# Attention value products issued for two key tiles at once, ahead of the sums of exp

## The chip, the cores and the metric

The kernel runs on one core of one Trainium2 chip. The metric is the device time of one execution in microseconds; smaller is better. Three executions before the change took 4082.6, 4084.34 and 4092.13 us; their median is 4084.34 us. A further execution was recorded by the hardware profiler; all rows of the profile come from it.

The engines are named as the profile names them: PE is TensorE (matmuls; PEld is its loading of weights), DVE is VectorE, ACT is ScalarE, POOL is GpSimd, SP is SyncE, which issues the DMAs.

## The reference

The program is a block of two layers over 1024 latent tokens and 256 context tokens, 1024 channels wide. Layer 0 mixes tokens with a bidirectional recurrence (RWKV-7), layer 1 with attention; each is followed by a squared-ReLU MLP. The change is in the attention of layer 1, which is cut here to what matters:

```python
sc = jnp.einsum('bqkgd,bskd->bkgqs', q, k_all) * scale   # 16 heads of 64, 4 key heads
p = jax.nn.softmax(sc, -1)                               # over 1024 + 256 keys
return jnp.einsum('bkgqs,bskd->bqkgd', p, v_all)
```

Only the 1024 latent tokens are queries; the keys are latent and context tokens, 1280 in all. So each head has 1024 queries, 10 key tiles of 128, and values 64 wide.

## The kernel before

All arithmetic is fp32. The dense layers split each operand into a high and a low part and make three matmuls of each product. Most of the time goes into these and into the recurrence; the attention of `phase_e` starts at about 2811 us of the span and ends at about 3253 us.

**Units and tiles.** `phase_e` (line 1319) goes over 16 units: 8 pairs of heads (`ct`) times 2 halves of 512 queries (line 1378). Within a unit it goes over the 10 key tiles (`kt`, line 1383). A key tile makes, in this order:

- scores: four matmuls, two for each head of the pair, into a PSUM tile of two banks (lines 1387 and 1388). The second of each pair has a 65th row that subtracts the row maximum, so exp needs no further operand;
- exp of the tile, on ScalarE, into an SBUF tile `p` (line 1391). `p` turns over five buffers (line 1389), so tile n+5 writes where tile n stood;
- the running sum of the `p` of a unit, `acc`, on GpSimd (lines 1396 and 1398; in the last pair of heads every third tile on VectorE);
- two "parts" (line 1402). In each part the generator `mx` is moved on by one (two while it catches up), and so is the generator `post`.

**Maxima.** `mx` is `maxima` (line 1200 on). It computes for later heads the row maxima that the scores subtract: one matmul pass into a PSUM bank (line 1224; two buffers) and one reduction on VectorE (lines 1226 and 1228). Once a unit it ends a head: a small reduction `mq` (line 1207), a transposing matmul `ps_mt` (line 1210), a ScalarE copy, and two DMAs. `MXLEAD = 6` and `MX0 = 4` set how far it runs ahead: in unit 0, from tile 2 on, it makes two steps in each part, later one, and in units 14 and 15 there are none left.

**Value products.** `values` (line 1341) makes the products of one key tile with the values: two calls, one for each head, whose outputs are 64 partitions each. They use half the columns of the array (`tile_position=(0, e * 64)`), and the profile shows four matmuls of the shape 128*64 for one key tile. They accumulate over the 10 key tiles in one PSUM bank, and ScalarE copies the result at the last one (line 1351). The tiles wait in the queue `late`; at line 1408 one is taken when more than `AVLAG = 2` stand there. So the products of tile n go out while tile n+2 is worked on.

**Sums and division.** `post` is `divided` (line 1353) for the unit before. It is started at tile `SUMAT = 3`. Its first step makes the matmul of `acc` with ones (line 1358), which also uses half the columns, and the first of eight reciprocals of 64 columns on VectorE (line 1361); each further part makes one more. Then come the product `ao * rec` (line 1363), a ScalarE copy (line 1366), and two parts later the low half `xl` (line 1369). The sum's PSUM buffer is one, shared with `ps_mt`.

**Order.** `line` (line 1335) chains what it is given: all matmuls of `phase_e` are one chain, and VectorE's reductions, reciprocals and products are another. Their order on the engine is therefore the order of the program's text. ScalarE and GpSimd follow their data. After the last unit, `late` is emptied and the last division is made (lines 1411 to 1413); then `phase_f` begins with the output projection.

Of the kernel before, what the change touches and what calls it, by code (L numbers as in the profile page):

```python
# [202 lines left out]
def drain(*gens):  # L203
    for g in gens:
        for _ in g:
            pass
# [980 lines left out]
def load_q(k, pools, ct):  # L1187

    nc, S, qs = k.nc, k.S, []
    for e in range(2):  # L1190
        o = slice(e * 64, e * 64 + 64)
        Q, Q2 = (pools[ct % len(pools)].tile([128, NL], F32R, name=f"{n}{e}", tag=f"{n}{e}") for n in ("Q", "M"))
        nc.sync.dma_start(out=Q[0:64].bitcast(F32), in_=S["qh"][ct][o])
        nc.sync.dma_start(out=Q[64:128].bitcast(F32), in_=S["ql"][ct][o])
        nc.sync.dma_start(out=Q2[0:64].bitcast(F32), in_=S["qh"][ct][o])
        qs.append((Q, Q2))
    return qs


def maxima(k, cts, qs, mp, pmx, psm, line):  # L1200


    nc, rows = k.nc, iter(())

    def row(ct, e, mc):
        m = mp.tile([128, 8], F32, name="mq", tag="mq")
        line(nc.vector.tensor_reduce(m, mc, AX.X, ALU.max), "v")
        yield
        ps = psm[0].tile([128, 512], F32, name="ps_mt", tag=psm[1])
        line(nc.tensor.matmul(ps[:8, :128], m, k.c["ident"], start=True, stop=True))  # L1210
        r = mp.tile([8, 128], F32R, name="mr", tag="mr")
        nc.scalar.activation(r, ps[:8, :128], AF.Copy, scale=-1.0)
        nc.sync.dma_start(out=k.S["mr"][ct][e].rearrange("(t q) -> t q", q=128), in_=r.bitcast(F32))
        nc.sync.dma_start(out=qs[ct][e][1][64:65].bitcast(F32), in_=k.S["mr"][ct][e:e + 1])

    for ct, e in itertools.product(cts, range(2)):
        Q, K_ = qs[ct][e][0], k.K1[ct // 2]
        mc = mp.tile([128, 8, 3], F32, name="mc", tag="mc")
        for t in range(0, 8, 2):
            for u, (t0, n) in [(u, b) for u in range(2) for b in TB[:2]] + [(None, TB[2])]:  # L1220
                ps = pmx[0].tile([128, 512], F32, name="ps_m", tag=pmx[1])
                for i in range(2) if u is None else (u,):
                    o = 256 * i if u is None else 0
                    line(nc.tensor.matmul(ps[:, o:o + n], Q[:, (t + i) * 128:(t + i) * 128 + 128], K_[:, t0:t0 + n], start=True, stop=True))  # L1224
                if u is None:
                    line(nc.vector.tensor_reduce(mc[:, t:t + 2, 2], ps.rearrange("p (a b) -> p a b", a=2), AX.X, ALU.max), "v")
                else:
                    line(nc.vector.tensor_reduce(mc[:, t + u, t0 // 512:t0 // 512 + 1], ps, AX.X, ALU.max), "v")  # L1228
                next(rows, None)
                yield  # L1230
        rows = row(ct, e, mc)
    drain(rows)
# [86 lines left out]
def phase_e(k, outs, qs, qp, mp):  # L1319

    tc, nc, S = k.tc, k.nc, k.S
    with ExitStack() as es:
        ep = es.enter_context(tc.tile_pool(name="ep", reuse_waits="tile", bufs=2))
        qp = (qp, *(es.enter_context(tc.tile_pool(name=f"qp{i}", reuse_waits="tile", bufs=1, side=side)) for i, side in ((1, "right"), (2, "left"))))
        pst = es.enter_context(tc.tile_pool(name="pst", reuse_waits="tile", bufs=2, space=PSUM))
        pmx = es.enter_context(tc.tile_pool(name="pmx", reuse_waits="tile", bufs=2, space=PSUM))
        psm = es.enter_context(tc.tile_pool(name="psm", reuse_waits="tile", bufs=1, space=PSUM))  # L1330
        pav = es.enter_context(tc.tile_pool(name="pav", reuse_waits="tile", bufs=1, space=PSUM))

        last = {}

        def line(i, e="pe"):

            if e in last:
                k.order(i, last[e])
            last[e] = i

        def values(u, p, kt, st):

            ct, half = u
            if kt == 0:
                st["av"] = pav.tile([128, 512], F32, name="ps_av", tag="av")
            for e in range(2):
                line(nc.tensor.matmul(st["av"][e * 64:e * 64 + 64], k.V[:, kt, ct // 2 * 64:ct // 2 * 64 + 64], p[:, e], start=(kt == 0), stop=(kt == 9),  # L1347
                                      tile_position=(0, e * 64)))
            if kt == 9:
                st["o"] = ep.tile([128, 512], F32, name="ao", tag="ao")  # L1350
                nc.scalar.copy(st["o"], st["av"])

        def divided(u, st):

            (ct, half), o = u, st["o"]
            ps = psm.tile([128, 512], F32, name="ps_su", tag="sm")
            for e in range(2):
                line(nc.tensor.matmul(ps[e * 64:e * 64 + 64], k.c["ones"][:, 0:64], st["acc"][:, e], start=True, stop=True, tile_position=(0, e * 64)))
            rec = ep.tile([128, 512], F32, name="rec", tag="rec", bufs=1)
            for j in range(0, 512, RW):  # L1360
                line(nc.vector.reciprocal(rec[:, j:j + RW], ps[:, j:j + RW]), "v")
                yield
            line(nc.vector.tensor_tensor(o, o, rec, ALU.mult), "v")
            sl = slice(half * 512, half * 512 + 512)
            hi, lo = outs[ct][0][:, sl], outs[ct][1][:, sl]
            nc.scalar.copy(hi, o)
            yield
            yield
            line(nc.vector.tensor_tensor(lo, o, hi.bitcast(F32), ALU.subtract), "v")
            if k.dbg and "ao" in k.O:  # L1370
                nc.sync.dma_start(out=k.O["ao"][ct][:, sl], in_=o)
            yield

        qs = {0: qs, **{ct: load_q(k, qp, ct) for ct in (1, 2)}}
        units = [(ct, half) for ct in range(KT) for half in range(2)]
        late, done, post, at, sent = collections.deque(), None, iter(()), 0, 0
        mx = maxima(k, range(1, KT), qs, mp, (pmx, "mx"), (psm, "sm"), line)
        for i, (ct, half) in enumerate(units):
            a, sl, st = ct // 2, slice(half * 512, half * 512 + 512), {}
            if half == 0:  # L1380
                if ct and ct + 2 < KT:
                    qs[ct + 2] = load_q(k, qp, ct + 2)
            for kt in range(10):
                ps = pst.tile([128, 2, 512], F32, name="ps_s", tag="s")
                kc = slice(kt * 128, kt * 128 + 128)
                for e, (Q, Q2) in enumerate(qs[ct]):
                    line(nc.tensor.matmul(ps[:, e], k.K1[a][:, kc], Q[:, sl], start=True, stop=False))  # L1387
                    line(nc.tensor.matmul(ps[:, e], k.K2[a][0:65, kc], Q2[0:65, sl], start=False, stop=True))  # L1388
                pool, tag = ((k.wp[1], "w_hi"), (k.wp[1], "w_lo"), (k.wp[0], "w_raw"))[(i * 10 + kt) % 5 % 3]
                p = pool.tile([128, 2, 512], F32, name="p", tag=tag)  # L1390
                nc.scalar.activation(p, ps, AF.Exp)  # L1391
                if kt == 0:
                    first = p
                elif kt == 1:
                    st["acc"] = ep.tile([128, 2, 512], F32, name="acc", tag="acc")
                    nc.gpsimd.tensor_tensor(st["acc"], first, p, ALU.add)
                else:
                    (nc.vector if ct == KT - 1 and kt % 3 == 2 else nc.gpsimd).tensor_tensor(st["acc"], st["acc"], p, ALU.add)  # L1398
                late.append(((ct, half), p, kt, st))
                if kt == SUMAT and i:  # L1400
                    post = divided(*done)
                for part in range(2):
                    at += 1
                    while sent < min(at + MXLEAD, 2 * (at - MX0)):
                        next(mx, None)
                        sent += 1
                    next(post, None)
                    if part == 0 and len(late) > AVLAG:
                        values(*late.popleft())
            done = (ct, half), st  # L1410
        while late:
            values(*late.popleft())
        drain(divided(*done))
# [3 lines left out]
AVLAG = 2  # L1417
# [63 lines left out]
```

## Time and profile before

| | us |
|---|---|
| median of three executions | 4084.34 |
| the profiled execution | 4093.04 |
| its span, first to last instruction | 4091.3 |
| PE busy in the span | 3611.4 (88%) |
| DVE busy | 2195.9 (54%) |
| ACT busy | 1512.4 (37%) |
| POOL busy | 1480.2 (36%) |
| value products, line 1347, 540 matmuls between 2811 and 3200 us | 145.8 busy |
| running sums, line 1398 on POOL, 109 adds there | 264.5 busy |

A row of the timeline gives the start, the duration, the engine, the line, the operation, output and inputs by the program's names, shapes, and how many were merged; in brackets the idle time of the engine before it and what ended it. Matmuls are pipelined, so the durations of neighbouring ones overlap: what one of them costs is read from start to start. A row of the windows gives a stretch, its length, the busy time and number of instructions of PE, PEld, DVE, ACT and POOL, the granted clock of TensorE as a share of full speed, the busy share of the DMA engines and GB/s.

### The profile page before, as it was taken

How to read it: one execution, taken by the hardware profiler on the slowest of the kernel's cores; microseconds unless marked ns; L12 is line 12 of the kernel's file. 1: busy time of each engine (PE TensorE's matmuls, PEld its weight loads, DVE VectorE, ACT ScalarE, POOL GpSimd, SP SyncE). 2: the span in 40 equal slices, each digit the busy share in tenths (PEclk: the TensorE clock that was granted, in tenths of full speed). 3: DMA queues.
4: the chain of work that ended last, by engine and by line, in shares of the span. 5: the costliest groups of instructions: out<-in, count | busy, mean ns of one | idle time of the engine just before them, and what ended most of it. 6: DMA issues, size and time to landing. Idle time of an engine off the chain costs nothing.

```text
span 4091.3 us, 70381 instructions
## 1 busy us (share of the span) xinstructions
PE 3611.4 (88%) x28100; PEld 2802.6 (69%) x28100; DVE 2195.9 (54%) x3707; ACT 1512.4 (37%) x3223; POOL 1480.2 (36%) x1387
## 2 busy tenths in 40 slices
PE   5999766883666779999999999889999999999998
PEld 3667654663566558788888888675444477888886
DVE  6337789998544665533333334657666453333334
ACT  5765555453444443411111112433444422221122
POOL 3114775765332423211111111124787612222221
PEclk7999866885878789999999999999999999999999
DMA  7456777777666553311111111432110111111112
GB/s 280 145 195 165 167 175 172 164 169 198 164 171 184 155 146 85 126 42 39 37 42 37 37 37 60 150 89 88 32 32 16 57 42 47 47 44 49 52 52 67
DMA packets 380279, 414.73 MB, mean 101 GB/s; under 512 B 150944, under 2 KB 280224, under 8 KB 374704
## 3 DMA queue, kind: packets, MB, share of 16 engines
q1 hardware_dynamic: 378992, 408.93, 36.4%
q8 instruction: 221, 3.62, 0.4%
q0 software_dynamic: 960, 1.31, 0.2%
q14 instruction: 106, 0.87, 0.1%
HBM read 294.99 MB, written 117.11 MB: 101 GB/s over the span
## 4 chain that ended last, share of the span: by engine, by line
PE 64%; DVE 11%; issue 4%; DMA 4%; ACT 1%; POOL 1%; SPq 1%; DVEq 0%; POOLq 0%; ACTq 0%
PE ps_pj L271 44%; PE ps_av L1347 4%; PE ps_s L868 3%; PE ps_m L1224 2%; PE ps_s L1387 2%; PE ps_pj L290 2%; PE ps_s L1388 2%; PE ps_y L877 1%; DVE To L712 1%; DVE Tn L713 1%; PE ps_x L848 1%; PE ps_x L854 1%; DMA wmod<-in_wmod 1%; DVE sgw L630 1%; DVE KT L653 0%
## 5 line engine op out<-in xcount | busy, mean ns | idle before, releaser
L255 POOL TENSOR_TENSOR w_lo<-w_raw,w_hi 128x512 fp32r<-128x512 f32 (+1 forms) x292 | 478.9, 1641 | 1677.7 <-ACT w_hi L253 1657.6
L271 PE MATMUL ps_pj<-xh,w_hi 128*128 128x512 f32 (+1 forms) x1712 | 626.3, 367 | 5.2 <-ACT w_hi L253 4.9
L271 PE MATMUL ps_pj<-xh,w_lo 128*128 128x512 f32 (+1 forms) x1712 | 618.3, 365 | 7.1 <-POOL w_lo L255 7.0
L271 PE MATMUL ps_pj<-xl,w_hi 128*128 128x512 f32 (+1 forms) x1712 | 622.6, 364 | 0.0
L1105 DVE SCALAR_TENSOR_TENSOR xr<-ps_pj,c_mod,xr 128x512 f32<-128x512 f32 (+1 forms) x368 | 251.8, 686 | 567.0 <-PE ps_pj L271 566.2
L253 ACT CAST w_hi<-w_raw 128x512 fp32r<-128x512 f32 (+1 forms) x292 | 216.6, 742 | 826.0 <-PE ps_pj L271 618.5
L271 PE MATMUL ps_pj<-hid_l,w_hi 128*128 128x512 f32 (+1 forms) x1280 | 474.4, 371 | 0.0
L271 PE MATMUL ps_pj<-hid_h,w_hi 128*128 128x512 f32 (+1 forms) x1280 | 473.1, 371 | 0.0
L271 PE MATMUL ps_pj<-hid_h,w_lo 128*128 128x512 f32 (+1 forms) x1280 | 469.8, 370 | 0.0
L1129 DVE TENSOR_TENSOR m_q<-m_r 128x512 f32<-128x512 f32 x160 | 183.6, 1149 | 415.5 <-ACT m_r L1127 415.2
L271 PEld LDWEIGHTS ps_pj<-xh,w_hi 128*128 128x128 f32 x1712 | 324.7, 190 | 59.9 <-ACT w_hi L253 6.6
L271 PEld LDWEIGHTS ps_pj<-xh,w_lo 128*128 128x128 f32 x1712 | 322.8, 190 | 61.0 <-POOL w_lo L255 9.9
L271 PEld LDWEIGHTS ps_pj<-xl,w_hi 128*128 128x128 f32 x1712 | 324.4, 190 | 51.5 <-issue 1.4
L1398 POOL TENSOR_TENSOR acc<-acc,p 128x1024 f32<-128x1024 f32 x122 | 295.5, 2423 | 58.6 <-ACT p L1391 54.2
L271 PEld LDWEIGHTS ps_pj<-hid_h,w_hi 128*128 128x128 f32 x1280 | 241.4, 189 | 44.3
L271 PEld LDWEIGHTS ps_pj<-hid_h,w_lo 128*128 128x128 f32 x1280 | 241.1, 188 | 43.8
L271 PEld LDWEIGHTS ps_pj<-hid_l,w_hi 128*128 128x128 f32 x1280 | 241.4, 189 | 43.2
L1391 ACT ACTIVATE p<-ps_s 128x1024 f32<-128x1024 f32 x160 | 163.8, 1024 | 231.1 <-PE ps_s L1388 229.2
L271 PE MATMUL ps_pj<-xhi,w_hi 128*128 128x512 f32 (+1 forms) x576 | 228.6, 405 | 15.2 <-ACT xhi L479 9.6
L271 PE MATMUL ps_pj<-xlo,w_hi 128*128 128x512 f32 (+1 forms) x576 | 227.2, 395 | 8.3 <-DVE xlo L480 8.1
L1228 DVE TENSOR_REDUCE mc<-ps_m 128x1 f32<-128x512 f32 x256 | 174.7, 690 | 100.8 <-PE ps_m L1224 97.0
L271 PE MATMUL ps_pj<-xhi,w_lo 128*128 128x512 f32 (+1 forms) x576 | 222.4, 388 | 3.7 <-POOL w_lo L255 3.7
(236 smaller groups left out, 6813.9 us busy)
## 6 DMA issues: line engine op xcount, KB each, us to landing
ST<-d_ST SPq DMA_DIRECT2D x40, 1152.0 KB
wmod<-in_wmod SPq DMA_DIRECT2D x32, 1024.0 KB
w_raw<-in_m SPq DMA_DIRECT2D x64, 512.0 KB
w_raw<-in_m SPq DMA_DIRECT2D x128, 256.0 KB
d_ST<-AR SPq DMA_DIRECT2D x160, 128.0 KB
d_LS<-KT SPq DMA_DIRECT2D x320, 64.0 KB
d_ST<-G SPq DMA_DIRECT2D x160, 128.0 KB
LS<-d_LS SPq DMA_DIRECT2D x80, 256.0 KB
```

Source lines behind the costliest of these rows:

```text
L253: nc.scalar.copy(hi, raw)
L255: getattr(nc, eng).tensor_tensor(lo, raw, hi.bitcast(F32), ALU.subtract)
L271: i = nc.tensor.matmul(ps[:, :n], w[:, sl], x[:, t0:t0 + n], start=a, stop=z)
L290: nc.tensor.matmul(ps[:, :n], w[:, sl], x[:, t0:t0 + n], start=a, stop=z)
L868: nc.tensor.matmul(pst[h * 64:h * 64 + 64, ct2, d, :], ls[:, h, ln, d, ct2, :, c], sv(h, ct2, d), start=True, stop=True, tile_position=(0, ...
L1105: k.nc.vector.scalar_tensor_tensor(x[:, t0:t0 + n], ps[:, :n], g, x[:, t0:t0 + n], ALU.mult, ALU.add)
L1129: nc.vector.tensor_tensor(q[:, :n], r[:, :n], r[:, :n], ALU.mult)
L1224: line(nc.tensor.matmul(ps[:, o:o + n], Q[:, (t + i) * 128:(t + i) * 128 + 128], K_[:, t0:t0 + n], start=True, stop=True))
L1228: line(nc.vector.tensor_reduce(mc[:, t + u, t0 // 512:t0 // 512 + 1], ps, AX.X, ALU.max), "v")
L1347: line(nc.tensor.matmul(st["av"][e * 64:e * 64 + 64], k.V[:, kt, ct // 2 * 64:ct // 2 * 64 + 64], p[:, e], start=(kt == 0), stop=(kt == 9) ...
L1391: nc.scalar.activation(p, ps, AF.Exp)
L1398: (nc.vector if ct == KT - 1 and kt % 3 == 2 else nc.gpsimd).tensor_tensor(st["acc"], st["acc"], p, ALU.add)
```

## The change

The call of `values` moves ahead of the step of `post`, and it is made at odd key tiles only, where it takes tiles from `late` until two are left. The matmuls, their number and their operands stay as they are.

```diff
                     while sent < min(at + MXLEAD, 2 * (at - MX0)):
                         next(mx, None)
                         sent += 1
+                    if part == 0 and kt % 2:
+                        while len(late) > AVLAG:
+                            values(*late.popleft())
                     next(post, None)
-                    if part == 0 and len(late) > AVLAG:
-                        values(*late.popleft())
```

On TensorE an even tile is then scores, maximum, maximum, and an odd tile is scores, maximum, value products of the two tiles two and three back, at tile 3 the sum of exp of the unit before, maximum. The last two tiles of a unit go out at tile 1 of the next, as they did at tiles 0 and 1; at the end the same two are left over.

## The prediction

> **What bounds the kernel now.** I read the page's span and chain first, then the busy time over the twelve middle units of the attention (the windows view), then TensorE's timeline there.
>
> ```profile
> span 4091.3 us, 70381 instructions
> ...
> 2858.84:3188.76 329.92, 329.92 (x1321) 160.72 (x1320) 226.93 (x372) 139.14 (x157) 261.84 (x109) 1.00 0.11 25
> ```
>
> The columns of the second row are the stretch, its length, busy time of PE, PEld, DVE, ACT and POOL, the granted clock, DMA. From the sum of exp of unit 1 to that of unit 13 TensorE is never idle (329.92 of 329.92 us, clock 1.00); VectorE has 227 and GpSimd 262 us of work. 12 units make one unit 27.49 us, a key tile 2.75. Everything outside the attention is untouched, so the whole question is what these 16 units become.
>
> Now one key tile on TensorE (start, duration, engine, line, what):
>
> ```profile
> 2958.04 0.40 PE L1224 MATMUL ps_m<-K,Q 128*128 128x256 f32 x2
> 2958.36 1.08 PE L1347 MATMUL ps_av<-p,Vat 128*64 128x512 f32 x4
> 2959.37 0.50 PE L1224 MATMUL ps_m<-K,Q 128*128 128x512 f32 x1
> 2959.71 0.39 PE L1387 MATMUL ps_s<-Q,K 128*128 128x512 f32 x1
> 2959.94 0.40 PE L1388 MATMUL ps_s<-M,K 65*128 65x512 f32 x1
> 2960.18 0.40 PE L1387 MATMUL ps_s<-Q,K 128*128 128x512 f32 x1
> 2960.42 0.40 PE L1388 MATMUL ps_s<-M,K 65*128 65x512 f32 x1
> 2960.66 0.40 PE L1224 MATMUL ps_m<-K,Q 128*128 128x512 f32 x1
> 2960.98 1.08 PE L1347 MATMUL ps_av<-p,Vat 128*64 128x512 f32 x4
> ```
>
> Durations overlap (the pipeline), so I count starts. Matmuls on the whole array (128*128) follow each other every 0.24 us (2959.71 to 2960.66 is four of them). The one ahead of the value products takes 0.32, the four value products on half the columns (128*64) 1.01, the maximum behind them 0.34. A block of value products that has another such block beside it is cheaper; the end of the attention and the step with the sum of exp show it:
>
> ```profile
> 3249.47 2.79 PE L1347 MATMUL ps_av<-p,Vat 128*64 128x512 f32 x12
> ```
>
> ```profile
> 2968.49 0.40 PE L1224 MATMUL ps_m<-K,Q 128*128 128x512 f32 x1
> 2968.82 1.08 PE L1358 MATMUL ps_su<-acc,c_ones 128*64 128x512 f32 x4
> 2969.73 1.03 PE L1347 MATMUL ps_av<-p,Vat 128*64 128x512 f32 x4
> 2970.68 0.50 PE L1224 MATMUL ps_m<-K,Q 128*128 128x512 f32 x1
> ```
>
> Three blocks in a row last 2.79, one lasts 1.08: each further block costs (2.79 - 1.08) / 2 = 0.855. The sum and its neighbour take 1.86 from start to the next maximum where two lone blocks take 2.02. So part of a lone block's price is the passage from the one shape to the other and back.
>
> **The change part by part.** *Fewer passages.* Maximum, lone block, maximum take 2958.04 to 2959.71 = 1.67; without passages they would take 2 x 0.24 + 0.855 = 1.33. One passage there and back costs 0.34. Before, a unit has 10 runs of half-column blocks (one for each key tile; the sum shares one with a value block). After, value products go out at odd tiles only, two tiles at once, and the sum at tile 3 stands behind them: 5 runs. That saves 5 x 0.34 = 1.70 a unit. Units 1 to 14: 14 x 1.70 = 23.8 us. No instruction is added or removed; no DMA moves.
>
> *Unit 0* loses. There the maxima catch up (four in a tile), and TensorE waits for VectorE:
>
> ```profile
> 2816.12 1.08 PE L1347 MATMUL ps_av<-p,Vat 128*64 128x512 f32 x4
> 2825.14 1.39 PE L1224 MATMUL ps_m<-K,Q 128*128 128x512 f32 x2 [7.94 <-DVE mc L1228]
> ```
>
> ```profile
> 2829.02 1.92 PE L1347 MATMUL ps_av<-p,Vat 128*64 128x512 f32 x4
> 2830.87 0.73 PE L1224 MATMUL ps_m<-K,Q 128*128 128x512 f32 x2
> ```
>
> ```profile
> 2825.00:2828.00 3.00, 2.86 (x6) 2.11 (x7) 1.97 (x4) 0.00 (x0) 1.70 (x1) 0.50 0.89 247
> ```
>
> The block of tile 0 stands ahead of that 7.94 us wait, for nothing. It moves behind it, where the clock is granted at half (0.50) and a block takes 2830.87 - 2829.02 = 1.85. Then tiles 4 and 6 have four maxima in a row with two PSUM buffers and no value products between them: the third waits for the first's reduction. By the durations below it comes 0.44 + 0.69 + 0.04 = 1.17 after the first and the fourth some 0.6 later, where 0.48 and 0.72 would do: about 1.1 of stall each. Against it stand 4 x 0.34 = 1.36 for its own four merged pairs and the short stalls that the catching-up has today. I take a loss of 2.0; the ends are a loss of 1.85 + 2.2 = 4 and a gain of 1.4.
>
> *VectorE.* Two tiles take 2 x 2.62 = 5.24 now and 4.90 then. VectorE's order stays (reduction, reciprocal, reduction, ...), but what it waits for moves.
>
> ```profile
> 2968.93 0.69 DVE L1228 TENSOR_REDUCE mc<-ps_m 128x1 f32<-128x512 f32 x1 [0.49 <-PE ps_m L1224]
> 2969.95 0.56 DVE L1361 RECIPROCAL rec<-ps_su 128x64 f32<-128x64 f32 x1 [0.33 <-PE ps_su L1358]
> 2971.23 0.69 DVE L1228 TENSOR_REDUCE mc<-ps_m 128x1 f32<-128x512 f32 x1 [0.72 <-PE ps_m L1224]
> 2971.84 0.55 DVE L1361 RECIPROCAL rec<-ps_su 128x64 f32<-128x64 f32 x1
> 2972.40 0.69 DVE L1226 TENSOR_REDUCE mc<-ps_m 128x2 f32<-128x512 f32 x1
> ```
>
> A reduction starts 0.44 after its maximum (2968.49 to 2968.93), 0.55 behind a run (2970.68 to 2971.23). Reduction to reciprocal is 0.61, reciprocal to reduction 0.56: in the tiles with reciprocals (3 to 6) VectorE needs 4 x 1.17 = 4.68 for two tiles. It fits 4.90 with 0.2 to spare, before 0.56. Where it is tight: at even tiles two maxima stand together. The second needs the buffer of the maximum behind the run, which started 0.34 + 0.95 + 0.24 = 1.53 earlier and is reduced 0.55 + 0.69 after its start, released 0.04 later (rows below: 2824.41 + 0.69 to 2825.14), 1.28 in all: spare 0.25. At tile 3 the first reciprocal comes 1.13 after the sum starts (2968.82 to 2969.95), the maximum 0.95 after it, and its reduction 1.13 + 0.56 - 0.95 = 0.74 behind the maximum: spare 0.06. So no stall, barely. What queues behind a late reduction is the maximum, and behind that, in TensorE's order, everything.
>
> *The lock between VectorE and GpSimd* is what can make VectorE late. A VectorE operation on two SBUF tiles waits for a running GpSimd add:
>
> ```profile
> 2821.59 2.34 POOL L1396 TENSOR_TENSOR acc<-p 128x1024 f32<-128x1024 f32 x1 [2.86 <-ACT p L1391]
> 2822.00 2.48 DVE L1308 TENSOR_TENSOR q_l<-q_n,q_h 128x512 fp32r<-128x512 f32 x1 [0.74 <-ACT q_h L1307]
> 2824.01 2.68 POOL L1398 TENSOR_TENSOR acc<-acc,p 128x1024 f32<-128x1024 f32 x1
> 2824.41 1.27 DVE L1228 TENSOR_REDUCE mc<-ps_m 128x1 f32<-128x512 f32 x2
> ```
>
> ```profile
> L1363 DVE TENSOR_TENSOR ao<-ao,rec x16: 679/681/2649, 2871.0 to 3258.0; 128x512 f32<-128x512 f32 x16
> L1369 DVE TENSOR_TENSOR xl<-ao,xh x16: 677/681/2097, 2874.0 to 3259.4; 128x512 fp32r<-128x512 f32 x16
> ```
>
> The q_l that is otherwise 0.69 took 2.48 and ended after the add; the queued add then waited (2.68 in place of 2.38). The two such operations of each unit, L1363 and L1369 at tiles 7 and 8, have a median of 0.681: today they fall into GpSimd's pauses. After, exp comes in pairs, the pauses move.
>
> ```profile
> 2960.91 1.02 ACT L1391 ACTIVATE p<-ps_s 128x1024 f32<-128x1024 f32 x1 [1.59 <-PE ps_s L1388]
> ```
>
> ```profile
> 2980.85 0.17 DVE L1207 TENSOR_REDUCE mq<-mc 128x8 f32<-128x24 f32 x1
> 2980.94 0.68 DVE L1363 TENSOR_TENSOR ao<-ao,rec 128x512 f32<-128x512 f32 x1
> ```
>
> By the count above L1363 falls due 10.6 after the sum starts (1.13 + 0.56 + 7 x 1.17 + 0.61, and 0.09 for the small L1207), that is 4.4 after the scores of tile 6 start (0.95 + 0.34 + 4.90 = 6.19 after the sum). The add of tile 6 begins about 2.4 after those scores (exp starts 1.20 after their first matmul, 2959.71 to 2960.91, and lasts 1.02) and ends at 4.8: a wait of 0.4, within the spare there. I take 0.1 a unit for it and the tight place together, 1.3 for units 1 to 13. The ends: 0, and a random phase. GpSimd will be busy 261.84 / 12 = 21.8 of 25.8 us, 85%; of a wait spread evenly over 0 to 2.4 the part beyond the spare of 0.25 is 2.15 x 2.15 / (2 x 2.4) = 0.96 on average, times 0.85 is 0.82, two of them 1.64 a unit, 21 us in all.
>
> The Trainium skill (SBUF — State Buffer, Who interferes with whom) says that a VectorE instruction with two SBUF inputs contends with a GpSimd instruction that reads SBUF, and that whoever issues first holds the port for its whole instruction. By that rule, the rows above agree (2.48 for 0.69); it is the rule that speaks against moving exp into pairs.
>
> *GpSimd and exp.* Two adds take 2 x 2.40 (261.84 / 109) = 4.80 of 4.90, nine of ten tiles have one: 21.8 of 25.8 a unit. It keeps up. The exp of tile n+5 reuses the p of tile n; an even tile's value products now run at n+3, still two tiles ahead. The copy of the accumulator gets a tile more. These cost nothing while that cover holds; without it a late p stops scores, and at most the 1.70 are gone.
>
> *Unit 15* and the end. The sum now starts 2 x 0.855 = 1.71 later in its step, and the reciprocals, L1363 and VectorE's add of tile 5 behind it:
>
> ```profile
> 3240.41 2.65 DVE L1363 TENSOR_TENSOR ao<-ao,rec 128x512 f32<-128x512 f32 x1
> 3242.98 1.21 DVE L1398 TENSOR_TENSOR acc<-acc,p 128x1024 f32<-128x1024 f32 x1
> ...
> 3244.71 2.37 POOL L1398 TENSOR_TENSOR acc<-acc,p 128x1024 f32<-128x1024 f32 x1 [2.21 <-ACT p L1391]
> ```
>
> GpSimd's add has 0.52 to spare after VectorE's (3244.19 to 3244.71). The scores of tile 3 come 0.34 + 0.855 = 1.2 earlier, the add 1.71 - 0.52 = 1.2 later against them, and the last sum and the next stage hang on it: 0, between a loss of 2.4 (one more add to wait for) and a gain of 1.7.
>
> **The sum.** 23.8 - 2.0 - 1.3 + 0 = 20.5 us. The profiled execution took 4093.04 (span 4091.3 and 1.74 around it): 4072.5. It lies 8.7 above the median of the runs, 4084.34: for the median 4084.34 - 20.5 = **4064**.
>
> **The rivals.** (a) *VectorE eats it.* The spare of 0.06 to 0.25 is missed and the lock comes at a random phase: 23.8 - 2 - 21 = 1 us of gain, 4084. For it: 85% of GpSimd's time; against it: the count that puts L1363 at the end of an add. (b) *Slower: both lock waits whole.* If L1363 and L1369 each start just behind a GpSimd add, in every unit, each waits 2.4, of which 2.15 reaches TensorE through the next maximum: 4.3 a unit against 1.70 saved, 13 x 2.6 = 34 lost, 2 more in unit 0 and 1.70 won in unit 14: 4084 + 34 = 4118. It decides once the two waits together pass 2.2 a unit. For it: 2649 and 2097 ns in the rows; against it: units repeat with one phase and the phase I find is another. (c) *It does not do what it says*: the passage is paid for each accumulation group rather than each change of shape, or GpSimd's pace sets the unit. Then nothing is saved, and unit 0 loses 2.0 + 1.36 = 3.4: 4088. Against it: the run of 12 and the sum beside a value block. (d) *Everything fits*: 23.8 + 1.4 + 1.7 = 27 us, 4057. (e) A run of half-column blocks might overlap its two column halves, so that each further block cost 0.43: 79 runs x 0.43 more, 34 us, 4030. Against it: 0.855 in the run of 12, whose blocks alternate the halves already.
>
> The Trainium skill (TensorEngine Tiling (Array Packing), Key Properties) says that different tiles can run matmuls in parallel; by that rule (e) would come. The trace disagrees, 0.855 for four matmuls.
>
> **How the numbers follow.** Forecast (gains of 13 to 24) 0.72, (d) 0.08, (a) 0.11, (b) 0.04, (c) 0.04, (e) 0.01. Runs of before lie between 4082.6 and 4092.13, and about 0.3% (12 us) is what a measurement tells from no change. Faster: 0.72 + 0.08 + 0.01 = 0.81. Same: (a) and (c), 0.15. Slower: 0.04. The range goes from (d) less 4 of scatter, 4053, to a gain of 6, 4078.
>
> **What would show it.** Right: pairs of value products as x8 of some 1.94, a unit of 25.8 between sums, the maxima behind one another 0.24 apart, L1363 still near 0.68 to 1.1. Wrong: TensorE idle before maxima on the release of a reduction in units 1 to 13, L1363 or L1369 with medians above 2, a marginal block above 1.0, a first unit longer by over 4.

## The result, and the profile after

The changed kernel takes 4055.01 us (median of four executions, 4051.38 to 4062.47), the kernel before 4086.53 beside it (4082.6 to 4092.13). The ratio of runs taken beside each other, which is not the quotient of the two medians, is 0.9934, with a 95% interval of 0.9917 to 0.9951: a gain of 20 to 34 us. A second timing, of both kernels unchanged, gave 4066.66 (five executions) against 4088.72 (fifteen): 0.9939, interval 0.9925 to 0.9952. The forecast was 4064, a gain of 20.5.

First the span and the windows view of the changed kernel from the sum of exp of unit 1 to that of unit 13, columns as before the change (stretch, length, busy time and instructions of PE, PEld, DVE, ACT, POOL, then granted clock, DMA share, GB/s).

```profile
span 4056.6 us, 70381 instructions
...
2850.12:3159.24 309.12, 309.12 (x1323) 168.92 (x1321) 219.81 (x372) 139.55 (x156) 262.98 (x109) 1.00 0.11 27
```

TensorE is still never idle in these twelve units and the clock is still 1.00, but they take 309.12 us in place of 329.92: 25.76 a unit in place of 27.49, 1.73 less. The instructions are the same. Now two key tiles and the step with the sum, in TensorE's timeline of the changed kernel (start, duration, engine, line, what).

```profile
2941.63 1.94 PE L1347 MATMUL ps_av<-p,Vat 128*64 128x512 f32 x8
...
2944.78 0.63 PE L1224 MATMUL ps_m<-K,Q 128*128 128x512 f32 x2
2945.24 0.39 PE L1387 MATMUL ps_s<-Q,K 128*128 128x512 f32 x1
...
2946.51 1.94 PE L1347 MATMUL ps_av<-p,Vat 128*64 128x512 f32 x8
...
2951.37 1.94 PE L1347 MATMUL ps_av<-p,Vat 128*64 128x512 f32 x8
2953.14 1.03 PE L1358 MATMUL ps_su<-acc,c_ones 128*64 128x512 f32 x4
```

The eight value matmuls stand as one run of 1.94 us, and from run to run are 2946.51 - 2941.63 = 4.88 us, where two tiles took 2 x 2.62 = 5.24 before. The maxima of an even tile stand together: two of them take 2945.24 - 2944.78 = 0.46, at the pace of 0.24 each that any full-array matmul has.

Where the whole gain lies is read from three places: the end of TensorE's long wait in unit 0, the first scores of unit 1, and the last sum of exp. For the changed kernel:

```profile
2815.11 1.39 PE L1224 MATMUL ps_m<-K,Q 128*128 128x512 f32 x2 [8.93 <-DVE mc L1228]
...
2840.82 0.40 PE L1387 MATMUL ps_s<-Q,K 128*128 128x512 f32 x1
...
3214.41 3.65 PE L1347 MATMUL ps_av<-p,Vat 128*64 128x512 f32 x16
3220.08 1.08 PE L1358 MATMUL ps_su<-acc,c_ones 128*64 128x512 f32 x4 [2.02 <-POOL acc L1398]
```

For the kernel before, whose wait ended at 2825.14:

```profile
2849.74 0.39 PE L1387 MATMUL ps_s<-Q,K 128*128 128x512 f32 x1
...
3253.33 1.08 PE L1358 MATMUL ps_su<-acc,c_ones 128*64 128x512 f32 x4 [1.06 <-POOL acc L1398]
```

From the wait to the last sum are 404.97 us in place of 428.19: the attention gains 23.2. From the last sum to the end of the span 836.52 in place of 837.97, 1.5 more. The change is therefore worth 24.7 us in these profiles. The spans differ by 34.7, and the other 10.0 lie ahead of the attention, where not a single instruction differs; the first experiment is about them.

| part | before | after | gain |
|---|---|---|---|
| end of the wait to first scores of unit 1 | 24.60 | 25.71 | -1.1 |
| first scores to sum of exp, unit 1 | 9.10 | 9.30 | -0.2 |
| sum of unit 1 to sum of unit 13 | 329.92 | 309.12 | 20.8 |
| sum of unit 13 to the last sum | 64.57 | 60.84 | 3.7 |
| last sum to the end of the span | 837.97 | 836.52 | 1.5 |

The second and the fourth row belong together: the sum of exp now stands behind one value block more (0.855) than before, which lengthens the way to the sum of unit 1 and shortens the way from that of unit 13.

### The profile page after: what moved, and what is told of

Read it like the earlier page. It is cut to its first block, busy times and chain, and to the rows that moved or that the text cites. A ratio compares the mean times of both kernels' runs of the same rounds, so it can differ in the third digit from the quotient of the medians.

```text
span 4056.6 us, 70381 instructions
## 1 busy us (share of the span) xinstructions
PE 3579.7 (88%) x28100; PEld 2807.2 (69%) x28100; DVE 2189.7 (54%) x3707; ACT 1510.9 (37%) x3223; POOL 1486.1 (37%) x1387
## 4 chain that ended last, share of the span: by engine, by line
PE 64%; DVE 11%; issue 4%; DMA 4%; ACT 1%; POOL 1%; SPq 0%; DVEq 0%; POOLq 0%; ACTq 0%
PE ps_pj L271 44%; PE ps_av L1347 4%; PE ps_s L868 3%; PE ps_m L1224 2%; PE ps_s L1387 2%; PE ps_pj L290 2%; PE ps_s L1388 2%; PE ps_y L877 1%; DVE To L712 1%; DVE Tn L713 1%; PE ps_x L854 1%; PE ps_x L848 1%; DVE sgw L630 1%; DVE KT L653 0%; DMA wmod<-in_wmod 0%
## 5 line engine op out<-in xcount | busy, mean ns | idle before, releaser
L830 POOL TENSOR_TENSOR T<-ST,c_qmask 128x256 f32<-128x256 f32 x160 | 118.2, 740 | 269.5 <-PE ps_x L854 187.0
```

Source lines behind the costliest of these rows:

```text
L830: k.nc.gpsimd.tensor_tensor(self.T, t.to_broadcast([128, 2, 4, 32]), k.c["qmask"].unsqueeze(1).to_broadcast([128, 2, 4, 32]), ALU.mult)
```

## The experiments

The theory, A: a unit is short by the passages between matmuls on half the columns and matmuls on the whole array, 0.34 us for each run of half-column blocks that is saved, and VectorE, GpSimd and the lock between them cost nothing as long as VectorE has its work done in 4.9 us for two tiles. The rivals: the order of the sums is what helps; the buffers of exp decide; VectorE is at its limit already.

**Both kernels again, unchanged: how much of the difference is the change?**

> The kernel before, unchanged, profiled a second time. The profiled execution of the changed kernel reached its attention 10 us earlier than that of the kernel before, though the change is behind that point. Theory A (scatter between executions): the second profile of the kernel before reaches its first scores anywhere within some 10 us of 2811, also near 2801, and its time lies anywhere between 4080 and 4095. Theory B (a property of the changed program): it reaches them again near 2811, within 2 us. Unit of the attention 27.49 us under both.

> The changed kernel, unchanged, timed in more rounds and profiled a second time. Theory A (scatter): its attention begins within some 10 us of 2801, and the difference to the kernel before comes nearer to the 23 us that the attention itself has gained in the first two profiles: ratio about 0.9943. Theory B (property of the program): attention begins again at 2801 within 2 us and the ratio stays at 0.992. Unit 25.76 us under both.

The kernel before came to 4086.74 against itself at 4088.72, ratio 0.9994 (0.9985 to 1.0004). The end of the long wait in unit 0 in the second profile of the kernel before, and in the second of the changed one:

```profile
2814.61 1.39 PE L1224 MATMUL ps_m<-K,Q 128*128 128x512 f32 x2 [7.60 <-DVE mc L1228]
```

```profile
2819.32 1.39 PE L1224 MATMUL ps_m<-K,Q 128*128 128x512 f32 x2 [8.81 <-DVE mc L1228]
```

The unchanged kernel now reaches the attention at 2814.61 where it took 2825.14 the first time, and the changed one at 2819.32 where it took 2815.11. So the 10.0 us are scatter of identical code, and in the second pair they have the other sign: spans 4080.9 and 4060.6 differ by 20.3, which is 25.0 less 4.7. Most of it arises in the recurrence: the 2560 matmuls of line 848 start between 1027.5 and 1479.0 us in the first profile of the kernel before and between 1027.3 and 1470.5 in its second, 451.5 against 443.2 us for the same instructions. From the wait to the last sum, on the other hand, the second profiles give 428.25 and 404.79, within 0.2 of the first. Below, a kernel is therefore judged by its unit (from sum to sum over twelve units), which repeats to 0.02 us: 27.493 and 27.493 before, 25.760 and 25.742 after. Several of the kernels below ran only once, under the profiler; their total time says little, their unit does.

**Value products on the whole array, in both orders: is it the change of shape?** If the gain is passages between shapes, it must vanish when the value products have the shape of everything else.

```diff
-                line(nc.tensor.matmul(st["av"][e * 64:e * 64 + 64], k.V[:, kt, ct // 2 * 64:ct // 2 * 64 + 64], p[:, e], start=(kt == 0), stop=(kt == 9),
-                                      tile_position=(0, e * 64)))
+                line(nc.tensor.matmul(st["av"], k.V[:, kt, ct // 4 * 128:ct // 4 * 128 + 128], p[:, e], start=(kt == 0 and e == 0), stop=(kt == 9 and e == 1)))
```

> The kernel before with value products on all 128 columns of the array (the values of two key heads side by side, both query heads into one PSUM bank, so the attention's result is another one). The sum of exp keeps its half columns. Theory (the price is the change of shape): of 10 runs of half-column blocks a unit 1 is left, 9 x 0.34 = 3.1 us less; the four matmuls of a tile follow each other at 0.235 in place of 0.214, 10 x 0.085 = 0.85 more: unit 27.49 - 3.1 + 0.85 = 25.3. Rival (the price is that of a block of value products that begins, whatever its shape): unit 27.5 to 28.3.

> The changed kernel with the same value products on all 128 columns (another result, as there). Theory (the price is the change of shape): of 5 runs 1 is left, 4 x 0.34 = 1.4 less, 0.85 more: unit 25.76 - 1.4 + 0.85 = 25.25, the same as in the other order of the products, so that the pairs bring nothing. Rival (a block that begins): 25.8 to 26.6, and the difference of 1.7 to the other order stays.

Both kernels leave out the separation of the two heads and so compute another attention; they serve for the time alone. They have one line less, so the scores stand in line 1386 and the sum in 1357. The windows of twelve units, with the order of before and with that of the change:

```profile
2866.53:3262.05 395.52, 395.52 (x1321) 231.53 (x1321) 227.09 (x372) 140.58 (x157) 261.06 (x109) 1.00 0.09 21
```

```profile
2864.79:3259.75 394.96, 394.96 (x1321) 231.26 (x1321) 219.80 (x372) 140.71 (x156) 260.07 (x109) 1.00 0.09 21
```

32.96 and 32.91 us a unit: the two orders differ by 0.05 where they differed by 1.73. Timed, they are level too (ratios to the kernel before 1.0201 and 1.0215, intervals 1.0184 to 1.0219 and 1.0201 to 1.0229). So the gain hangs on the change of shape. The size was missed: 25.3 was expected and 33 came. TensorE's timeline of the first of the two says why.

```profile
2952.59 0.40 PE L1224 MATMUL ps_m<-K,Q 128*128 128x256 f32 x2
2952.83 1.88 PE L1347 MATMUL ps_av<-p,Vat 128*128 128x512 f32 x4
2954.14 0.79 PE L1224 MATMUL ps_m<-K,Q 128*128 128x512 f32 x1
2954.77 0.40 PE L1386 MATMUL ps_s<-Q,K 128*128 128x512 f32 x1
```

From the maximum to the scores are 2.18 us, and less the two maxima of 0.24 the block costs 1.70, about twice the 0.855 of a block on half columns. The passage is gone: a maximum ahead of it takes 0.24, not 0.32. The four matmuls of a half-column block, then, run two at a time, one on each half of the columns, and in the whole-array form one after the other. The timeline merges neighbouring records; taken singly, over the first 0.4 us of a block (2958.40 to 2958.80 in the kernel before, 2952.84 to 2953.24 in this one), they show it (count, shortest, median and longest in ns, first and last start):

```profile
L1347 PE MATMUL ps_av<-p,Vat x2: 643/643/643, 2958.4 to 2958.4; 128*64 128x512 f32 x2
```

```profile
L1347 PE MATMUL ps_av<-p,Vat x1: 592/592/592, 2952.8 to 2952.8; 128*128 128x512 f32 x1
```

Two half-column matmuls start within 0.02 us of each other and the next two 0.48 later; on the whole array one starts every 0.43 (2952.83, 2953.26, 2953.68). A pair takes about the time of one, so it is not that fewer columns make a matmul shorter. With that price the units come out: 27.49 - 9 x 0.34 + 10 x 0.855 = 32.98 and 25.76 - 4 x 0.34 + 10 x 0.855 = 32.95 (the sum of exp keeps its one passage).

The rows of weight loading (PEld) suggest what a passage consists of. Between matmuls of one shape the next weights are loaded 0.2 us ahead (in the changed kernel a load at 2948.72 for the scores that start at 2948.95). At a change of shape the load starts only with its matmul: at 2951.37 for the value products, at 2948.37 for the maximum behind a run. One such load takes 0.19 us for 128 columns and 0.13 for 64, together 0.32 of the 0.34. This is read from the rows; no run varied it.

**The order of the sums by itself.** The kernel before with its value products ahead of the step of `post`, one tile at a time.

```diff
+                    if part == 0 and len(late) > AVLAG:
+                        values(*late.popleft())
                     next(post, None)
-                    if part == 0 and len(late) > AVLAG:
-                        values(*late.popleft())
```

> One part of the change alone: value products ahead of the sum of exp, but still at every tile, one tile at a time. Runs of half-column blocks stay 10 a unit. Theory: unit 27.49, no gain; the first reciprocal 0.86 later. Rival (the place of the sums matters by itself): a unit shorter or longer by more than 0.2.

```profile
2844.95:3174.86 329.91, 329.91 (x1322) 160.72 (x1320) 225.49 (x372) 139.20 (x157) 261.87 (x108) 1.00 0.11 25
```

27.49 us a unit, as before the change. The order gives nothing by itself; the 1.73 come with taking two tiles at once.

**One passage more.** In the changed kernel the sum goes to tile 2, where no value products stand.

```diff
-SUMAT = 3
+SUMAT = 2
```

> The changed kernel with the sum of exp started at tile 2 in place of 3, where no value products stand beside it: 6 runs of half-column blocks a unit. Theory (each run costs one passage of 0.34, whichever block is in it): unit 25.76 + 0.34 = 26.10. Rival (only value products pay): 25.76.

The windows and the sum's surroundings in TensorE's timeline:

```profile
2852.89:3166.08 313.19, 313.19 (x1321) 167.02 (x1320) 229.21 (x372) 139.22 (x157) 264.77 (x108) 1.00 0.12 26
```

```profile
2956.96 0.39 PE L1224 MATMUL ps_m<-K,Q 128*128 128x512 f32 x1
2957.28 1.08 PE L1358 MATMUL ps_su<-acc,c_ones 128*64 128x512 f32 x4
2958.29 0.50 PE L1224 MATMUL ps_m<-K,Q 128*128 128x512 f32 x1
```

26.10 a unit, 0.34 more than 25.76, with the sum between two maxima as a lone block. One run more costs 0.34, as counted.

**One passage fewer, twice.** If 0.34 were all, four runs a unit would be better than five. Two places for the run that is left out:

```diff
-                    if part == 0 and kt % 2:
+                    if part == 0 and (kt in (1, 3, 5, 9) or i == 0 and kt == 2):
```

> The changed kernel with value products at tiles 1, 3, 5 and 9 only (2, 2, 2 and 4 tiles at once): 4 runs a unit, and in unit 0 one block at tile 2, ahead of the long wait. Theory: unit 25.76 - 0.34 = 25.42, 15 units 5 us, unit 0 about 1 us: about 6 us faster than the changed kernel. Rival (the five buffers of exp run out: at tile 9 exp waits for the value products of tile 4, and scores behind it): unit 25.76 or more.

```diff
-                    if part == 0 and kt % 2:
+                    if part == 0 and (kt in (1, 3, 5, 7) or (i, kt) in ((0, 2), (15, 9))):
```

> As the four-run kernel, but the four tiles stand together at tile 1 of the next unit (value products at tiles 1, 3, 5 and 7, of 4, 2, 2 and 2 tiles), so that the pair at tile 7 stays, behind which VectorE catches up; unit 0 has one block at tile 2, the last unit its pair at tile 9. Theory (in the first four-run kernel TensorE waited for VectorE at tile 7 because no value products stood there; each run costs 0.34): no wait at tile 7, unit 25.75 - 0.34 = 25.41, unit 0 shorter by 0.9 as there, about 6 us less than the changed kernel in the attention, some 0.9925 of the kernel before. Rival (tiles 8, 9 and 0 without value products starve the five buffers of exp or the two of the maxima): unit 25.75 or more.

Both missed, with 26.96 and 26.97 us a unit in place of 25.4 (ratios to the kernel before 0.9979, 0.997 to 0.9987, and 0.9963, 0.995 to 0.9977). The windows and the waits (total us, times, longest) of the first:

```profile
2856.92:3180.44 323.52, 311.94 (x1322) 169.13 (x1320) 228.87 (x372) 139.58 (x156) 264.19 (x109) 1.00 0.11 25
```

```profile
PE ps_mt L1210 <- DVE mq L1207: 7.0, 12, 0.6
PE ps_m L1224 <- DVE mc L1226: 4.5, 12, 0.4
```

The rows of one unit of the first, where no value products stand at tile 7:

```profile
2946.36 0.40 PE L1224 MATMUL ps_m<-K,Q 128*128 128x512 f32 x1
2947.13 0.50 PE L1224 MATMUL ps_m<-K,Q 128*128 128x512 f32 x1 [0.37 <-DVE mc L1226]
2948.21 0.39 PE L1210 MATMUL ps_mt<-c_ident,mq 128*8 128x128 f32 x2 [0.58 <-DVE mq L1207]
```

And the waits of the second:

```profile
PE ps_m L1224 <- DVE mc L1228: 7.7, 12, 0.7
PE ps_s L1388 <- DMA M<-d_mr: 3.6, 5, 0.9
```

TensorE, which was never idle before, now is for 323.52 - 311.94 = 11.6 us in the first, each time on VectorE, once a unit at a maximum and once at `ps_mt`. In the second it waits once a unit, 0.64 us, for the release of a reduction, and in five of the twelve units for the row maxima that come by DMA. Neither waits for the buffers of exp, the rival of the first. The rival of the second named the two buffers of the maxima as well, and that is what came: the wait is for one of them. Where a run is left out, four maxima or more follow each other with only scores between them, and VectorE, which reduces them, gets behind. The idle time is 0.96 of the 1.54 us that the first came out too long; the other 0.57 counts as busy time, because durations overlap and hide part of a wait. From start to start the rows above show it: the second maximum comes 0.77 behind the first in place of 0.24, `ps_mt` 1.08 behind that in place of 0.43 (in the changed kernel 2963.86 to 2964.29), and the next two maxima of that unit take 0.73 (2949.56 to 2950.29) in place of 0.48. That is 1.43 too much, nearly the whole. How the second divides was not settled.

**How much spare VectorE has.** In the changed kernel the reciprocals are made longer, with 96 and with 192 columns in place of 64, by making columns twice or three times over.

```diff
-                line(nc.vector.reciprocal(rec[:, j:j + RW], ps[:, j:j + RW]), "v")
+                line(nc.vector.reciprocal(rec[:, j:min(j + 96, 512)], ps[:, j:min(j + 96, 512)]), "v")
```

(The second has 192 at both places.)

> The changed kernel with each reciprocal on 96 columns in place of 64 (they overlap; the result is the same), to take VectorE's spare away. A reciprocal then takes between 0.55 and 0.83. Prediction's count: two tiles with reciprocals need 4 x (0.61 + 0.72) = 5.3 of VectorE at the middle of that, TensorE 4.90; so VectorE sets tiles 3 to 6, and the unit is 25.76 + 2 x 0.4 = 26.6. Rival (VectorE has much to spare, since TensorE's waits on it are 0 in the changed kernel's trace): 25.76.

> The changed kernel with each reciprocal on 192 columns. At 6.1 ns a column (0.549 at 64, 0.743 at 96) one takes 1.33; reduction and reciprocal follow each other at 0.54 + 1.24 = 1.78 when VectorE is behind, 7.1 for two tiles against TensorE's 4.89. Theory (VectorE is hidden up to 4.89 for two tiles, and 4 x 1.20 = 4.80 was still hidden): now it shows, four tiles with reciprocals become up to 2 x 2.2 longer, unit 28 to 30. Rival (VectorE never decides here): 25.8.

Windows of the first, and its row of the reciprocals (shortest, median, longest in ns):

```profile
2857.73:3167.85 310.12, 310.12 (x1323) 169.67 (x1321) 227.26 (x372) 139.48 (x156) 262.68 (x109) 1.00 0.12 26
```

```profile
L1361 DVE RECIPROCAL rec<-ps_su x128: 541/743/759, 2858.8 to 3235.8; 128x96 f32<-128x96 f32 x112, 128x64 f32<-128x64 f32 x16
```

Windows and waits of the second:

```profile
2851.87:3221.20 369.33, 340.55 (x1322) 172.60 (x1320) 279.64 (x372) 139.61 (x156) 257.31 (x109) 0.95 0.10 22
```

```profile
PE ps_m L1224 <- DVE mc L1228: 24.0, 34, 1.3
```

At 96 columns a reciprocal is 0.743 long, 0.19 more, four of them for two tiles 0.78, and the unit is 25.84, only 0.08 longer. By the prediction's count, with a spare of 0.2 for two tiles, it would have been 26.6. At 192 columns (1.342 each, by the same row of that kernel) the unit is 30.78, a little above the 28 to 30 expected, and TensorE waits for reductions: 2.40 us a unit are idle (369.33 less 340.55, over 12). The rest of the 5.02 lies in busy time, part of it at a lower clock (0.95), and was not divided. VectorE has more to spare than counted, and it does have a limit. The count is corrected by its timeline in the changed kernel, at a place where it is behind:

```profile
2956.41 0.55 DVE L1361 RECIPROCAL rec<-ps_su 128x64 f32<-128x64 f32 x1
2956.87 0.63 DVE L1228 TENSOR_REDUCE mc<-ps_m 128x1 f32<-128x512 f32 x1
2957.42 0.54 DVE L1361 RECIPROCAL rec<-ps_su 128x64 f32<-128x64 f32 x1
```

When VectorE has nothing to wait for, a reduction comes 0.46 behind a reciprocal and a reciprocal 0.55 behind a reduction, 1.01 for the two and 4.04 for two tiles, not 4.68. At 96 columns the same steps are 0.55 and 0.65, as the timeline of that kernel shows:

```profile
2965.30 0.63 DVE L1228 TENSOR_REDUCE mc<-ps_m 128x1 f32<-128x512 f32 x1
2965.85 0.74 DVE L1361 RECIPROCAL rec<-ps_su 128x96 f32<-128x96 f32 x1
2966.50 0.63 DVE L1228 TENSOR_REDUCE mc<-ps_m 128x1 f32<-128x512 f32 x1
```

That makes 4.80 for two tiles, which just fits the 4.88 there are, and the unit hardly moved.

**Unit 0's block back ahead of its wait.**

```diff
-                    if part == 0 and kt % 2:
+                    if part == 0 and (kt % 2 or (i, kt) == (0, 2)):
```

> The changed kernel, but in unit 0 the value products of tile 0 go out alone at tile 2 again, ahead of the long wait of the maxima, as in the kernel before. From the end of that wait to the sum of exp of unit 1 the changed kernel takes 35.0 us, the kernel before 33.7 (its sum then stands one block of 0.855 and one passage earlier). Theory of the prediction (the block behind the wait runs at half the clock and costs 1.85): 35.0 - 1.85 + what the pair at tile 3 loses, 33.2 to 33.7. Rival (the clock recovers, or the maxima hide the block): 34.0 to 35.0. All later units 25.75; in the whole time at most 2 us, under what can be told from no change.

TensorE's timeline of this kernel:

```profile
2819.75 1.39 PE L1224 MATMUL ps_m<-K,Q 128*128 128x512 f32 x2 [7.85 <-DVE mc L1228]
...
2853.83 1.03 PE L1358 MATMUL ps_su<-acc,c_ones 128*64 128x512 f32 x4
```

From the end of the wait to the sum of unit 1 are 34.08 us, in the changed kernel 2850.12 - 2815.11 = 35.01: the block behind the wait cost 0.93, not the 1.85 of the prediction, nor nothing. In the whole time (a single execution, 4062.59) 0.9 us can't be seen, so nothing says that this kernel is faster as a whole.

## Why the prediction was right

**Fewer passages: right.** Five runs saved at 0.34 make 1.70; the unit lost 1.73. That the change of shape is what costs is shown by four runs: no difference between the two orders where the shapes are alike, none from the order of the sums alone, and +0.34 for one more run, in which the lone block is not a value product.

**VectorE and the lock: the term of 1.3 was nothing.** 0.1 a unit had been set down for it, and 1.73 against 1.70 leaves no room for it. TensorE is busy for all of the 309.12 us; a short wait could still lie under overlapping durations, but the unit has no room for one. The spare of 0.06 and 0.25 was worked out with the distances at which VectorE runs when it waits for its inputs; when behind it runs closer, and then needs 4.04 of the 4.88 us of two tiles, not 4.68. The wait at the lock itself came, a little larger than forecast. The two operations on SBUF in the changed kernel:

```profile
L1363 DVE TENSOR_TENSOR ao<-ao,rec x16: 692/1248/1803, 2860.4 to 3224.8; 128x512 f32<-128x512 f32 x16
L1369 DVE TENSOR_TENSOR xl<-ao,xh x16: 693/734/2786, 2863.7 to 3226.1; 128x512 fp32r<-128x512 f32 x16
```

L1363 has a median of 1.248 where it had 0.681: 0.57 more, where 0.4 was forecast and 0.68 to 1.1 named as the sign of being right. In one unit it lasts from 2963.39 to 2964.62, and GpSimd's running add ends at 2964.1, 0.5 before it: it waits for the add. The spare hides this. So (a) and (b) did not come: neither operation meets a whole add as a rule (2.4 each for (b)).

**GpSimd and exp: cost nothing, as said.** Exp now does wait for buffers that GpSimd still reads, as the waits of the changed kernel from 2850 to 3160 us show (the kernel before has none of them in its twelve units), but no wait of TensorE follows from it, so (c) with GpSimd setting the pace did not come either.

```profile
ACT p L1391 <- POOL acc L1396: 9.2, 11, 0.8
```

**Unit 0: right in kind, half in size.** A loss of 2.0 was forecast and 1.1 came. The windows view of the changed kernel over the first tile behind the wait and over the run behind that:

```profile
2815.11:2818.99 3.88, 3.88 (x9) 2.67 (x9) 2.15 (x4) 0.74 (x1) 1.55 (x1) 0.50 0.97 245
2818.99:2821.31 2.32, 2.32 (x9) 0.60 (x8) 0.97 (x2) 0.28 (x1) 1.90 (x1) 0.79 1.03 212
```

The prediction priced the block at half clock, 1.85, but the clock is granted again while the run lasts (0.50, then 0.79). The run takes 2821.31 - 2818.99 = 2.32 to the next maximum, and the experiment puts the block at 0.93. The difference, 0.92, is the whole of the error. The stalls at tiles 4 and 6 came as worked out, the third maximum 1.19 after the first in both (forecast 1.17); at tile 4:

```profile
2822.82 0.88 PE L1224 MATMUL ps_m<-K,Q 128*128 128x512 f32 x3
2824.01 1.09 PE L1224 MATMUL ps_m<-K,Q 128*128 128x512 f32 x2 [0.30 <-DVE mc L1228]
2824.94 0.40 PE L1387 MATMUL ps_s<-Q,K 128*128 128x512 f32 x1
```

Four maxima take 2.12 us to the next scores where four at 0.24 would take 0.96, so the stall is 1.16, though the row in brackets says 0.30: the rest lies under the durations, which overlap.

**The end: 0 forecast, 1.7 gained.** For the two units outside the twelve 3.4 less 0.1 was due, and 3.7 less 0.2 came, although the last sum waited longer for the add (2.02 in place of 1.06). The 1.5 behind the last sum were not in the forecast. The traces say where they lie. The output projection starts 1.56 behind the last sum in place of 2.19 (0.6 gained). Its third matmul waits 1.7 us in both kernels; in the kernel before the clock behind this wait is 0.56 for 3.27 us, and in the changed kernel it is 1.00, so that the same eight steps take 1.95 (1.3 gained). Some 0.5 is lost again later. The second profiles show the same (clock 0.57 and 1.00), so this is not scatter; why the clock holds in one case and not in the other was not tested. The prediction had no term for it, so this part of the gain is luck.

**Rival (e) fell, but its reason was wrong.** The prediction held against it that four matmuls of a block take 0.855 "whose blocks alternate the halves already", and concluded that the halves don't overlap. The whole-array kernels show the opposite: the overlap was already inside the 0.855, since the same four matmuls take 1.70 without it, and the single records of the kernel before show the pairs. The forecast for a further block stands, but the sentence that "the trace disagrees" with the Trainium skill (TensorEngine Tiling (Array Packing), Key Properties) was a misreading: tiles do run in parallel here, 0.855 against 1.70.

**The sum.** 20.8 for the twelve units (forecast 12 x 1.6 = 19.2), -1.1 in unit 0, -0.2 up to the first sum, 3.7 and 1.5 at the end: 24.7 in place of 20.5. It lies between the forecast and (d), 27. The medians give 31.5 the first time and 22.1 the second; scatter of the size seen ahead of the attention is enough for that, though the executions that were only timed show no stages. The mechanism and the size of the main term were right. That the first median, 4055.01, came out 9 below the forecast and only 2 above the end of the range is scatter as far as the traces tell: 24.7 less than 4086.53 would be 4062.

## What to carry to other kernels

Where matmuls of two shapes alternate on a full TensorE, price the passage by comparing a lone block with one in a row, and gather blocks of one shape; but leave something between the maxima for the engine that reduces them, since one run fewer still cost 1.2 us a unit. An engine's need is counted at the pitch (the distance from start to start) it has when it is behind, not when it waits for inputs. Judge a change by the stage it is in, from one landmark to another: here the stage repeated to 0.2 us while the way to it scattered by 10.

## What the runs showed of the hardware

- **Half-column fp32 blocks overlap.** Two matmuls on the two halves of the columns take 0.855 us for 512 columns of data, where the whole-array form of the same two takes 1.70. The merged rows of the timeline hide this; the single records show it, two starting within 0.02 us of each other.
- **VectorE's pitch is below its durations when it is behind**: 0.55 behind a reduction of 0.63, 0.46 behind a reciprocal of 0.55. The reciprocal from PSUM took 0.549, 0.743 and 1.342 us at 64, 96 and 192 columns.
- **The clock recovers within a run of matmuls**, 0.50 and then 0.79 in 2.3 us, and short waits can lower it: in the second kernel with four runs two waits of 0.63 and 0.67 us stand 1.9 us apart (to 2977.60 and 2979.46), and the granted clock is 0.55 from 2980 to 2982, 0.60 to 2984, and 1.00 behind that. The length of a wait alone does not decide it: over its twelve units that kernel has 0.99, with a wait of some 0.6 in each, and around the last sum three waits of 1.06, 1.11 and 1.69 us are followed by 0.56 in the kernel before, three of 2.02, 0.47 and 1.70 by 1.00 in the changed one.
- **Identical code scattered by 10 us ahead of the attention**, mostly in the recurrence (451.5 and 443.2 us for the same matmuls), while the attention repeated to 0.2.
